# Decay sums of the state-space heads: six matmuls per head, or one table broadcast by DMA

## The chip, the cores and the metric

The kernel runs on one core of a Trainium2 chip, as one program launched once. The metric is the device time of that core in microseconds (us). The engines are TensorE (PE; PEld is its weight load), VectorE (DVE), ScalarE (ACT), GpSimd (POOL) and SyncE (SP), which issues every DMA here.

## The reference, cut to what matters

One layer over 256 prompt tokens and 64 sample tokens, D_MODEL 4096. After an input projection there are 16 attention-like heads ("stick-breaking") and 32 state-space heads of width 64; then an output projection, a gate projection and norms. What the change touches is the decay inside the state-space heads:

```python
dt = softplus(dt_raw + dt_bias)
a = -exp(a_log)
acum = cumsum(dt * a, axis=tokens)          # per head
diff = acum[l] - acum[s]
decay = exp(where(s <= l, diff, -inf))
wts = (C B^T)[l, s] * decay[l, s] * dt[s]
y[l] = sum_s wts[l, s] * x[s]               # + decayed initial state + d_skip * x
```

The reference does this in chunks of 64 with a state between them; the kernel takes all 256 prompt tokens at once, and the 64 sample tokens with the state that is handed in. A prompt and a sample of a head together make a [128 x 512] tile of decays: rows are source tokens s, columns are (s 0-127, l 0-255) | (s 128-255, l 128-255) | (sample s, sample l) | (64 sample l for the initial state).

## The kernel before, in words

**Projections.** All large matrices are taken in column blocks of 256. `project` goes through eight groups of 512 rows; for each, `weights` (L152 to L160) loads a 512 KB tile `raw` by SP, ACT rounds it to `whi` (L158), DVE makes the rest `wlo` (L159), and PE does three float32r matmuls per 128x128 weight tile (L163, L164, L165: `whi*xhi`, `whi*xlo`, `wlo*xhi`), 24 matmuls for each group of rows and block. There are 4 buffers for `raw` and 3 each for `whi` and `wlo`.

**Work behind the projections.** Everything else is written as generators that are put on a list by `start`. After each group of rows, `project` calls `tick`, which takes each generator to its next `yield`. So the small matmuls of the heads stand on PE in blocks between two groups of 24 large matmuls. The engines' programs are put in order ahead of time by the framework's scheduler, and each engine runs its own in order.

**The order of the program.** First three blocks of q, k and v together while x is loaded and transposed (`load_h`; x tiles come from `big()`); then the gate of head pair 0, during which `steps` runs; then four times `ssd_pair`: B and C (two groups of 256 columns), then per group x and z. Head pairs 1 to 7 of the attention follow, then the output projection and the gate.

**State-space heads.** `steps` (L469) makes dt of every token and head, `dta` = dt * a as [128 tokens x 3 windows x 32 heads], its two parts `dtah` and `dtal` in float32r, the decays to the end `dend` and the whole windows' decay `bd`. `ssd_heads` (L614) is started once for each of 16 units of two heads. Its stages: transpose x (`natural`, L557) and scale it to `xdt` and `xde`; per head six DVE multiplications (L636) of the mask `le` by a column of `dtah` or `dtal`, into `gh` and `gl`; the state's matmuls (L640 to L642, once per unit); per head six float32r matmuls (L651 to L656) that sum `gh` and `gl` over tokens with the triangular `gt_r` and the all-ones `ones_r` into a PSUM tile `df`; exp on ACT (L658); times `cb` = masked B^T C on DVE (L659). A tick later y: for each of the unit's two heads four float32 matmuls (L665 to L668) of 64 output rows; head 0 writes PSUM partitions 0 to 63, head 1 partitions 64 to 127. Each float32 matmul stands in the trace as two, called passes here.

`big()` gives [128 x 512] tiles from a ring of 7, used by `load_h`, `steps`, the attention heads and the state-space heads; `small()` gives narrower ones from a ring of 13 with the tag `w`.

Of the kernel before, what the change touches and what calls it, by code (L numbers as in the profile page):

```python
# [30 lines left out]
# Token windows of 128 columns: prompt 0-127, prompt 128-255, and one whose last 64 are the sample.  # L31
WIN = ((0, 128), (128, 256), (192, 320))
# In a row with three convolution columns between prompt and sample.
# [8 lines left out]
def hymba_step(  # L42
# [17 lines left out]
    # what lives in one half of the kernel: the mixers, or the projections behind them  # L60
# [9 lines left out]
    def big(dtype=F32):  # L70
        return pool["wk"].tile([P, 512], dtype, tag="b", name="b", bufs=7)
# [31 lines left out]
    # keeps row > column  # L103
# [5 lines left out]
    # two identities of 32 on top of each other  # L109
# [3 lines left out]
    # Upper bound of the attention scores: huge where a key may be seen, hugely negative elsewhere.  # L113
    # Columns: keys 0-127 x prompt | cache x sample | keys 128-255 x prompt 128-255 | sample keys x sample
    cap = const1.tile([P, 512], F32, name="cap")
    G.memset(cap, -MASKED)
    for c0, n, base in ((0, 128, 0), (320, 128, 0), (448, 64, 64)):
        # keeps column + base - row > 0
        G.affine_select(out=cap[:, c0:c0 + n], in_=cap[:, c0:c0 + n], compare_op=ALU.is_gt,
                        fill=MASKED, base=base, pattern=[[1, n]], channel_multiplier=-1)  # L120
    G.memset(cap[0:64, 448:512], MASKED)
    # 1 where row <= column, by blocks: (0,0) | (0,1) all | (1,1) | sample
# [29 lines left out]
    def weights(src, kg, c0, nk=KG):  # L152
        """nk row tiles of NCOL columns, split exactly into two parts of 12 bits."""
        raw = wp.tile([P, nk, NCOL], F32, tag="raw", name="raw", bufs=4)
        SY.dma_start(raw, src[kg * nk * P:(kg + 1) * nk * P, c0:c0 + NCOL].rearrange("(k p) c -> p k c", p=P))
        hi = wp.tile([P, nk, NCOL], F32R, tag="whi", name="whi")
        lo = wp.tile([P, nk, NCOL], F32R, tag="wlo", name="wlo")
        S.copy(hi, raw)  # L158
        V.tensor_sub(lo, raw, hi.bitcast(F32))  # L159
        return hi, lo  # L160
# [6 lines left out]
    # Work behind a projection, as generators that pause between their stages; projections take  # L167
    # them one step further with each group of rows, so that the tensor engine finds their operands ready.
# [19 lines left out]
    def project(specs, acts, nk=KG, order=range(NG), ticks=True):  # L188
        """Products of column blocks (matrix, first column, PSUM tag), two feature tiles each, with
        all tokens. acts(kg) gives the kg-th group of rows of the activations, in two parts."""  # L190
# [22 lines left out]
    def rsqrt_mean(out, total, n, shape):  # L213
        """out = (total / n + EPS) ** -0.5, with one step of Newton's method."""
# [8 lines left out]
    def factor_of(sqs, n):  # L223
        """The norm's factor of each token, on all partitions, from partial sums of squares."""
# [13 lines left out]
    class Squares:  # L238
        """Sum over `count` feature tiles of squares; the last one stays apart."""
# [3 lines left out]
        def add(self, make):  # L243
            """make(tile, soon) squares the next feature tile."""
# [80 lines left out]
    def gate_in(g):  # L325
        """-g, bounded below as the exponential's argument is above."""
# [4 lines left out]
    def gate_out(es, vals, outs):  # L331
        """out = val / (1 + exp(-g)) for each e of gate_in(g); the quotient by one step of Newton's method."""
# [3 lines left out]
        for e, r in zip(es, rs):  # L336
            # 1 + e, scaled into the logarithm's range
            S.activation(r, e, AF.Ln, scale=2.0 ** -62, bias=tiny)  # L338
# [16 lines left out]
    def put_u(i, ap_mul):  # L355
        """Unit i (16 of each mixer) of the mixed output before its norm."""
# [10 lines left out]
    def to_rows(t, h, dst_p, dst_s, n):  # L367
        """A head's keys or values, back in rows of tokens."""
# [50 lines left out]
    def stick(h, i, q, k, vn, ck, cv, gss):  # L419
# [15 lines left out]
        # softplus(z), and log sigmoid(z) over z  # L435
# [27 lines left out]
    dtah = const1.tile([P, 3, SSDH], F32R, name="dtah")  # L463
    dtal = const1.tile([P, 3, SSDH], F32R, name="dtal")
# [4 lines left out]
    def steps():  # L469
        """dt of each token and head (tokens on partitions), dt * a, and decays."""  # L470
# [8 lines left out]
        # columns of the weights: their first parts, their second parts, nothing  # L479
# [24 lines left out]
        # softplus(r) = max(r, 0) + log1p(e), e = exp(-|r|); log1p(e) = 2 atanh(e / (2 + e))  # L504
# [18 lines left out]
        S.copy(dtah, dta)  # L523
        V.tensor_sub(dtal, dta, dtah.bitcast(F32))
        yield 3
# [12 lines left out]
    def conv(acc, ct, out):  # L538
        """Causal convolution and SiLU of a channel tile; out has 323 columns, the sample's at XS."""
# [74 lines left out]
    def ssd_heads(u, i, xt, made, ys):  # L614
        """Heads 2u and 2u+1: their outputs (transposed) and final states."""
# [14 lines left out]
        wts = []  # L630
        for half in range(2):
            h = 2 * u + half
            gh, gl = big(F32R), big(F32R)
            for out, part in ((gh, dtah), (gl, dtal)):
                for c0, c1, w in ((0, 256, 0), (256, 384, 1), (384, 448, 2)):
                    V.tensor_scalar_mul(out[:, c0:c1], le[:, c0:c1], part[:, w, h:h + 1].bitcast(F32))  # L636
            yield 1
            if half == 0:
                st = aux()
                PE.matmul(st[:, 0:P], xde[:, 0, :], bn[:, 0, :], start=True, stop=False)  # L640
                PE.matmul(st[:, 0:P], xde[:, 1, :], bn[:, 1, :], start=False, stop=True)
                PE.matmul(st[:, P:2 * P], xde[:, 2, :], bn[:, 2, :], start=True, stop=True)  # L642
                so = small((P, 2, P))
                S.copy(so[:, 0, :], st[:, 0:P])
                V.scalar_tensor_tensor(out=so[:, 1, :], in0=h0, scalar=bd[:, u:u + 1], in1=st[:, P:2 * P],
                                       op0=ALU.mult, op1=ALU.add)
                for k, dst in enumerate((ssd_prompt, ssd_sample)):
                    SY.dma_start(dst[0, 0].rearrange("(u a) p n -> (a p) u n", a=2)[:, u, :], so[:, k, :])
            df = aux()
            # sums of dt * a over s < r <= l; the last 64 columns over all r <= l of the sample  # L650
            PE.matmul(df[:, 0:448], gt_r, gh[:, 0:448], start=True, stop=False)  # L651
            PE.matmul(df[:, 0:448], gt_r, gl[:, 0:448], start=False, stop=False)
            PE.matmul(df[:, 128:256], ones_r, gh[:, 256:384], start=False, stop=False)
            PE.matmul(df[:, 128:256], ones_r, gl[:, 256:384], start=False, stop=True)
            PE.matmul(df[:, 448:512], ones_r, gh[:, 384:448], start=True, stop=False)
            PE.matmul(df[:, 448:512], ones_r, gl[:, 384:448], start=False, stop=True)  # L656
            wt = big()
            S.activation(wt, df, AF.Exp)  # L658
            V.tensor_mul(wt, wt, cb)  # L659
            wts.append(wt)  # L660
        yield 1
        y = aux()
        for half, wt in enumerate(wts):
            ph = slice(half * 64, half * 64 + 64)
            PE.matmul(y[ph, 0:256], xdt[:, 0, ph], wt[:, 0:256], start=True, stop=False)  # L665
            PE.matmul(y[ph, 128:256], xdt[:, 1, ph], wt[:, 256:384], start=False, stop=True)  # L666
            PE.matmul(y[ph, 256:320], xdt[:, 2, ph], wt[:, 384:448], start=True, stop=False)
            PE.matmul(y[ph, 256:320], h0t[:, ph], wt[:, 448:512], start=False, stop=True)  # L668
# [158 lines left out]
    def put_pair(fp, gates, es):  # L827
        """Gated embedding of two feature tiles, with the norm's weight."""
# [9 lines left out]
    def to_token_rows(fp, t):  # L838
        """Of each four feature tiles: 512 columns of each half of the prompt's rows, and the sample's rows
        with the first two tiles, then with the last two."""  # L840
# [9 lines left out]
        if half:  # L850
            pt = aux()
            for i in range(2):
                # a transpose writes from the first row on: the last two's, then the first two's over their head
# [8 lines left out]
    # units: a group's rows of half of the prompt, or two groups' rows of the sample  # L862
# [27 lines left out]
    def some_residuals(count):  # L890
        """The first units' residuals, into SBUF ahead of time."""
# [91 lines left out]
```

## Time and profile before

| | before |
|---|---|
| time, median of 3 runs | 2769.45 us (2768.79 to 2770.16) |
| the profiled execution's span | 2768.3 us |
| PE busy | 2741.7 us, 99% |
| DVE busy | 1450.8 us, 52% |
| ACT busy | 1110.9 us, 40% |
| POOL busy | 241.5 us, 9% |
| DMA | 414 MB, 150 GB/s, q1 at 50.2% of 16 engines |

For the profiled execution the page gives the span alone, from the first instruction to the last; the median of the timed runs is 1.15 us longer. A busy engine is one with at least one instruction in it. PE's matmuls overlap, so its time is read from one start to the next, not from the duration of one.

### The profile page before, as it was taken

To read this page: it belongs to the slowest core of one execution; us is meant where nothing else is said; L and a number is where in the kernel's file an instruction comes from. 1 tells how busy PE (TensorE), PEld (TensorE's weight loads), DVE (VectorE), ACT (ScalarE), POOL (GpSimd) and SP (SyncE) were. 2 spreads that over 40 slices of the span, in tenths; PEclk is the share of its full clock that TensorE was granted. 3 is DMA by queue.
4 is the path that set the end of the run, shared out by engine and by line. 5 is a ranking of instruction groups with operands and counts; after the bars stand their busy time and mean duration, and the time that the engine had idled before them with its cause. 6 is when DMAs were issued, how large, how long until landed. Compare 5 with 4: busy or idle time off the path is not lost.

```text
span 2768.3 us, 45230 instructions
## 1 busy us (share of the span) xinstructions
PE 2741.7 (99%) x18710; PEld 2713.2 (98%) x18710; DVE 1450.8 (52%) x2155; ACT 1110.9 (40%) x1551; POOL 241.5 (9%) x327
## 2 busy tenths in 40 slices
PE   9999999999999999999999999999999999999998
PEld 8999999999999999999999999999999989999997
DVE  4566666666666534435354453653333386454453
ACT  5443334433344333424333343543333354444441
POOL 0000010010000000000000000000101032121110
PEclk9999999999999999999999999999999999999997
DMA  7645454454454554555555455555444464444442
GB/s 236 194 120 145 132 149 138 127 164 127 143 148 134 149 153 143 151 149 146 152 143 157 140 150 161 168 162 159 148 150 152 137 191 147 150 144 151 149 142 84
DMA packets 419183, 414.13 MB, mean 150 GB/s; under 512 B 21792, under 2 KB 410784, under 8 KB 418976
## 3 DMA queue, kind: packets, MB, share of 16 engines
q1 hardware_dynamic: 418976, 411.24, 50.2%
q8 instruction: 146, 2.39, 0.3%
q14 instruction: 61, 0.50, 0.0%
HBM read 390.64 MB, written 20.55 MB: 149 GB/s over the span
## 4 chain that ended last, share of the span: by engine, by line
PE 96%; issue 1%; POOL 1%; DMA 1%; DVE 0%; ACT 0%; SPq 0%; DVEq 0%; POOLq 0%; ACTq 0%
PE acc L163 30%; PE acc L165 29%; PE acc L164 29%; POOL ug L817 1%; PE px L876 1%; DMA raw<-in_w_in_dram 1%; PE aux L665 1%; PE aux L372 0%; PE aux L492 0%; PE aux L557 0%; PE aux L847 0%; PE aux L453 0%; PE aux L666 0%; PE aux L426 0%; PE aux L651 0%
## 5 line engine op out<-in xcount | busy, mean ns | idle before, releaser
L163 PE MATMUL acc<-ahi,whi 128*128 128x320 f32 x5632 | 1757.6, 312 | 0.0
L165 PE MATMUL acc<-ahi,wlo 128*128 128x320 f32 x5632 | 1741.6, 309 | 3.6 <-DVE wlo L159 3.6
L164 PE MATMUL acc<-alo,whi 128*128 128x320 f32 x5632 | 1742.2, 309 | 1.3 <-DVE alo L819 1.2
L159 DVE TENSOR_TENSOR wlo<-raw,whi 128x1024 fp32r<-128x1024 f32 (+1 forms) x720 | 888.9, 1236 | 1119.6 <-ACT whi L158 1109.6
L158 ACT CAST whi<-raw 128x1024 fp32r<-128x1024 f32 (+1 forms) x720 | 747.1, 1038 | 1369.3 <-PE acc L164 1328.0
L165 PEld LDWEIGHTS acc<-ahi,wlo 128*128 128x128 f32 x5632 | 1058.5, 188 | 5.4 <-DVE wlo L159 5.4
L164 PEld LDWEIGHTS acc<-alo,whi 128*128 128x128 f32 x5632 | 1059.7, 188 | 2.5 <-DVE alo L819 2.3
L163 PEld LDWEIGHTS acc<-ahi,whi 128*128 128x128 f32 x5632 | 1059.3, 188 | 2.5
L252 POOL TENSOR_TENSOR stat<-stat,w 128x320 f32<-128x320 f32 x88 | 117.5, 1335 | 596.8 <-ACT w L779 404.6
L236 POOL TENSOR_TENSOR w<-ug 128x320 f32<-128x320 f32 x26 | 31.1, 1197 | 947.2 <-DVE ug L457 687.5
L335 ACT ACTIVATE w<-w 128x320 f32<-128x320 f32 (+1 forms) x96 | 45.1, 470 | 101.6 <-DVE w L328 101.5
L342 DVE SCALAR_TENSOR_TENSOR w<-w 128x320 f32<-128x320 f32 (+1 forms) x96 | 51.3, 541 | 16.3 <-ACT w L340 16.3
L236 POOL TENSOR_TENSOR w<-w 128x320 f32<-128x320 f32 x29 | 31.1, 1071 | 296.4 <-DVE w L346 296.4
L550 DVE SCALAR_TENSOR_TENSOR w<-w,vec 128x323 f32<-128x323 f32 x96 | 53.1, 553 | 2.1
L338 ACT ACTIVATE w<-w,tiny 128x320 f32<-128x320 f32 (+1 forms) x96 | 52.3, 560 | 2.9
L340 ACT ACTIVATE w<-w,shift 128x320 f32<-128x320 f32 (+1 forms) x96 | 52.2, 559 | 1.4
L344 DVE SCALAR_TENSOR_TENSOR w<-w 128x320 f32<-128x320 f32 (+1 forms) x96 | 49.6, 529 | 1.2
L545 POOL COPY ctail<-w 128x3 f32<-128x3 f32 x32 | 6.1, 190 | 328.3 <-DVE w L543 328.3
L328 DVE TENSOR_SCALAR w<-acc 128x320 f32<-128x320 f32 x32 | 15.6, 488 | 24.8 <-PE acc L165 24.7
L817 POOL TENSOR_TENSOR ug<-ug,two 128x320 f32<-128x320 f32 x16 | 23.7, 1486 | 43.2 <-DVE ug L816 43.2
L818 ACT CAST ahi<-ug 128x320 fp32r<-128x320 f32 x32 | 14.4, 461 | 25.8 <-POOL ug L817 22.4
L636 DVE TENSOR_SCALAR b<-le,dtah 128x256 fp32r<-128x256 f32 (+2 forms) x96 | 24.7, 292 | 0.0
(270 smaller groups left out, 1476.7 us busy)
## 6 DMA issues: line engine op xcount, KB each, us to landing
raw<-in_w_in_dram SPq DMA_DIRECT2D x448, 512.0 KB, 3.7
raw<-in_w_out_dram SPq DMA_DIRECT2D x128, 512.0 KB, 3.6
raw<-in_w_ple_gate_dram SPq DMA_DIRECT2D x128, 512.0 KB, 3.6
xt_dram<-ug SPq DMA_DIRECT2D x8, 640.0 KB, 6.2
two<-xt_dram SPq DMA_DIRECT2D x16, 320.0 KB, 3.3
b<-in_x_prompt_dram SPq DMA_DIRECT2D x16, 256.0 KB, 4.7
out_dram<-nat SPq DMA_DIRECT2D x32, 128.0 KB, 1.8
raw<-in_w_ple_proj_dram SPq DMA_DIRECT2D x16, 256.0 KB, 2.7
```

Source lines behind the costliest of these rows:

```text
L158: S.copy(hi, raw)
L159: V.tensor_sub(lo, raw, hi.bitcast(F32))
L163: PE.matmul(out, whi, xhi, start=start, stop=False)
L164: PE.matmul(out, whi, xlo, start=False, stop=False)
L165: PE.matmul(out, wlo, xhi, start=False, stop=stop)
L236: G.tensor_mul(sq, t, t)
L252: G.tensor_add(self.sum, self.sum, sq)
L338: S.activation(r, e, AF.Ln, scale=2.0 ** -62, bias=tiny)
L340: S.activation(r, r, AF.Exp, scale=-1.0, bias=shift)
L342: V.scalar_tensor_tensor(out=e, in0=e, scalar=1.0, in1=r, op0=ALU.add, op1=ALU.mult)
L550: V.scalar_tensor_tensor(out=c, in0=ext[:, j:j + XE], scalar=vec3[:, j * 32 + ct:j * 32 + ct + 1], in1=c, op0=ALU.mult, op1=ALU.add)
L817: (G if j % 2 else V).tensor_add(m, m, xt[:, j % 2, :])
```

## The change

Three things are changed in the state-space heads, and one buffer count.

1. `steps` sums `dta` over tokens once for all 32 heads (three float32 matmuls with a triangular matrix `tri`, in which sums start anew every 32 tokens), writes the [32 x 512] table to DRAM (`sums_dram`), and makes a table `off` of [128 x 32 heads x 16] offsets by twenty more small float32 matmuls, in four stages with a `yield` ahead of each.
2. `ssd_heads` no longer makes `gh` and `gl` and no longer runs the six matmuls per head. A DMA on SP broadcasts a head's row of 512 sums to all 128 partitions of a tile `t`; DVE subtracts `off` (one value per 32 columns) and takes the minimum with 0; then exp in place, times `cb` in place.
3. The y matmuls of the two heads alternate, piece by piece, where before all four of head 0 stood ahead of those of head 1.
4. `big()` has 6 buffers, was 7. The comments are dropped.

```diff
     def big(dtype=F32):
-        return pool["wk"].tile([P, 512], dtype, tag="b", name="b", bufs=7)
+        return pool["wk"].tile([P, 512], dtype, tag="b", name="b", bufs=6)
...
-    dtah = const1.tile([P, 3, SSDH], F32R, name="dtah")
-    dtal = const1.tile([P, 3, SSDH], F32R, name="dtal")
+    off = const1.tile([P, SSDH, 16], F32, name="off")
+    sums_dram = dram.tile([SSDH, 512], F32, name="sums_dram")
...
-        S.copy(dtah, dta)
-        V.tensor_sub(dtal, dta, dtah.bitcast(F32))
-        yield 3
+        tri = small((P, P))
+        V.tensor_copy(tri, le[:, 0:P])
+        for c in range(1, 4):
+            G.memset(tri[0:32 * c, 32 * c:32 * c + 32], 0.0)
+        yield 1
+        pt = aux()
+        PE.matmul(pt[0:32, 0:128], dta[:, 0, :], tri, start=True, stop=True)
+        PE.matmul(pt[0:32, 128:256], dta[:, 1, :], tri, start=True, stop=True)
+        PE.matmul(pt[0:32, 256:320], dta[:, 2, :], tri[:, 64:128], start=True, stop=True)
+        sums = big()
...
+        SY.dma_start(sums_dram, sums[0:32, :])
+        pt = aux()
+        acc = pt.rearrange("p (k h) -> p k h", k=16)
+        after = small((P, P))
+        V.tensor_scalar_mul(after, gt, -1.0)
+        for c in range(4):
+            mat = small((P, P))
+            V.tensor_copy(mat, le[:, 0:P])
+            if c:
+                V.tensor_copy(mat[0:32 * c, :], after[0:32 * c, :])
+            early = small((P, P))
+            G.memset(early, 0.0)
+            if c:
+                G.memset(early[0:32 * c, :], -1.0)
+            yield 1
+            PE.matmul(acc[:, c, :], mat, dta[:, 0, :], start=True, stop=True)
+            PE.matmul(acc[:, 8 + c, :], mat, dta[:, 1, :], start=True, stop=True)
+            if c >= 2:
+                PE.matmul(acc[:, 10 + c, :], mat, dta[:, 2, :], start=True, stop=True)
+                PE.matmul(acc[:, 12 + c, :], early, dta[:, 2, :], start=True, stop=True)
+            PE.matmul(acc[:, 4 + c, :], after, dta[:, 0, :], start=True, stop=False)
+            PE.matmul(acc[:, 4 + c, :], early, dta[:, 1, :], start=False, stop=True)
+        V.tensor_copy(off, acc.rearrange("p k h -> p h k"))
...
+        sums = []
         for half in range(2):
-            gh, gl = big(F32R), big(F32R)
-            for out, part in ((gh, dtah), (gl, dtal)):
-                for c0, c1, w in ((0, 256, 0), (256, 384, 1), (384, 448, 2)):
-                    V.tensor_scalar_mul(out[:, c0:c1], le[:, c0:c1], part[:, w, h:h + 1].bitcast(F32))
...
-            PE.matmul(df[:, 0:448], gt_r, gh[:, 0:448], start=True, stop=False)
-            PE.matmul(df[:, 0:448], gt_r, gl[:, 0:448], start=False, stop=False)
-            PE.matmul(df[:, 128:256], ones_r, gh[:, 256:384], start=False, stop=False)
-            PE.matmul(df[:, 128:256], ones_r, gl[:, 256:384], start=False, stop=True)
-            PE.matmul(df[:, 448:512], ones_r, gh[:, 384:448], start=True, stop=False)
-            PE.matmul(df[:, 448:512], ones_r, gl[:, 384:448], start=False, stop=True)
-            wt = big()
-            S.activation(wt, df, AF.Exp)
-            V.tensor_mul(wt, wt, cb)
+            t = big()
+            SY.dma_start(t, sums_dram[2 * u + half:2 * u + half + 1, :].broadcast_to([P, 512]))
+            sums.append(t)
+        yield 1
...
+        for half, t in enumerate(sums):
+            t16 = t.rearrange("p (k c) -> p k c", k=16)
+            V.tensor_sub(t16, t16, off[:, 2 * u + half, :].unsqueeze(2).broadcast_to([P, 16, 32]))
+            V.tensor_scalar_min(t, t, 0.0)
+            S.activation(t, t, AF.Exp)
+            V.tensor_mul(t, t, cb)
         yield 1
         y = aux()
-        for half, wt in enumerate(wts):
-            ph = slice(half * 64, half * 64 + 64)
-            PE.matmul(y[ph, 0:256], xdt[:, 0, ph], wt[:, 0:256], start=True, stop=False)
...
+        for a, b, c, w, first_, last_ in pieces:
+            for half, wt in enumerate(sums):
+                ph = slice(half * 64, half * 64 + 64)
+                PE.matmul(y[ph, a:b], h0t[:, ph] if w == 3 else xdt[:, w, ph], wt[:, c:c + b - a],
+                          start=first_, stop=last_)
```

On PE, around one unit of two heads, before: y of the unit that ends (b_2867 and b_2915 are its two heads' weights, aux_2968 is y), the state's matmuls of the next unit, and the sums of that unit's first head. The large matmuls ahead and behind are left out.

```order
L665 MATMUL aux_2968<-b_2867,nat_2805 64x256
L666 MATMUL aux_2968<-b_2867,nat_2805 64x128
L667 MATMUL aux_2968<-b_2867,nat_2805 64x64
L668 MATMUL aux_2968<-b_2867,w_2486 64x64
L665 MATMUL aux_2968<-b_2915,nat_2805 64x256
...
L640 MATMUL aux_2980<-nat_2447,nat_2923 128x128
...
L651 MATMUL aux_2989<-b_2930,gt_r_102 128x448
...
L656 MATMUL aux_2989<-b_2931,ones_r_89 128x64
```

On PE of the changed kernel, the state's matmuls of a unit and, 24 large matmuls later, its y (b_2871 and b_2873 are the two heads' weights).

```order
L676 MATMUL aux_2905<-nat_2505,nat_2864 128x128
L677 MATMUL aux_2905<-nat_2505,nat_2864 128x128
L678 MATMUL aux_2905<-nat_2505,nat_2864 128x128
...
L700 MATMUL aux_2952<-b_2871,nat_2863 64x256
L700 MATMUL aux_2952<-b_2873,nat_2863 64x256
L700 MATMUL aux_2952<-b_2871,nat_2863 64x128
L700 MATMUL aux_2952<-b_2873,nat_2863 64x128
L700 MATMUL aux_2952<-b_2871,nat_2863 64x64
L700 MATMUL aux_2952<-b_2873,nat_2863 64x64
```

The rows L651 to L656 have no counterpart, and the rows of y alternate between the two heads. L640 to L642, now L676 to L678, stand in a block of their own.

On DVE, in `steps` of the changed kernel, the chain that makes `dta` (L515 and L516 are one step of a polynomial, L522 writes `dta`; the seven steps before and behind are left out). The copies L529, L545, L549 and L551 make `tri`, `after` and the matrices `mat`.

```order
L529 COPY w<-le 128x128
L515 TENSOR_TENSOR w<-w 128x96
L545 TENSOR_SCALAR w<-gt 128x128
...
L549 COPY w<-le 128x128
L516 TENSOR_SCALAR w<-w 128x96
L551 COPY w<-w 32x128
...
L522 SCALAR_TENSOR_TENSOR dta<-dt,w 128x32 x3
L539 COPY b<-aux 32x192
L540 COPY b<-aux 32x64
L159 TENSOR_TENSOR wlo<-raw,whi 128x1024 x2
```

Nine such copies now stand between the first row of the chain and `dta`, none before. On PE the first matmul that reads `dta` stands at the same place as before: 72 large matmuls behind L500 (now L501).

On SP, in the first projection, a piece of the difference: `b` are the x tiles, `dsk` is the d_skip vector spread over partitions (64 rows of 16 single values, twice), `raw` the weights.

```order
-L400 DMA keep<-in_cache_v_dram 128x128
-L478 DMA dsk<-in_d_skip_dram 64x16x1
-L155 DMA raw<-in_w_in_dram 128x4x256
-L293 DMA xt_dram<-ug 128x1280
...
-L478 DMA dsk<-in_d_skip_dram 64x16x1
-L155 DMA raw<-in_w_in_dram 128x4x256 x2
...
+L400 DMA keep<-in_cache_v_dram 128x128
+L479 DMA dsk<-in_d_skip_dram 64x16x1 x2
+L155 DMA raw<-in_w_in_dram 128x4x256
+L293 DMA xt_dram<-ug 128x1280
```

With one x tile less to load early, the second `dsk` moves up to stand right behind the first; before, two x tiles' worth of loads and two `raw` stood between them.

## Rows read from the trace of the kernel before

**Rows 1.** Page: the span, and each engine's busy time, share and instructions.

```profile
span 2768.3 us, 45230 instructions
PE 2741.7 (99%) x18710; PEld 2713.2 (98%) x18710; DVE 1450.8 (52%) x2155; ACT 1110.9 (40%) x1551; POOL 241.5 (9%) x327
```

**Rows 2.** Windows: the state-space stage (PE, PEld, DVE, ACT, POOL; clock, DMA).

```profile
186.00:934.00 748.00, 748.00 (x5201) 738.12 (x5199) 496.12 (x976) 295.49 (x397) 63.92 (x161) 1.00 0.49 140
```

**Rows 3.** Timeline of PE, two heads' sums (start, duration, engine, line, operation).

```profile
267.90 0.45 PE L651 MATMUL aux<-b,gt_r 128*128 128x448 f32 x1
...
268.75 0.39 PE L163 MATMUL acc<-ahi,whi 128*128 128x320 f32 x1
...
272.35 0.37 PE L651 MATMUL aux<-b,gt_r 128*128 128x448 f32 x1
...
273.12 0.55 PE L557 MATMUL aux<-ident,keep 128*128 128x128 f32 x3
```

**Rows 4.** Timeline of PE, y of one unit (x2: both passes in one row).

```profile
277.12 0.65 PE L665 MATMUL aux<-b,nat 128*64 128x256 f32 x2
...
277.82 0.22 PE L667 MATMUL aux<-b,nat 128*64 128x64 f32 x1
277.82 0.43 PE L665 MATMUL aux<-b,nat 128*64 128x256 f32 x1
...
277.93 0.28 PE L668 MATMUL aux<-b,w 128*64 128x64 f32 x2
...
278.64 0.28 PE L668 MATMUL aux<-b,w 128*64 128x64 f32 x2
278.85 0.49 PE L640 MATMUL aux<-nat 128*128 128x128 f32 x2
```

**Rows 5.** Timeline of DVE and PE at the end of `steps` (brackets: idle before, releaser).

```profile
176.15 1.23 DVE L159 TENSOR_TENSOR wlo<-raw,whi 128x1024 fp32r<-128x1024 f32 x1 [0.44 <-ACT whi L158]
...
181.73 0.39 DVE L521 SCALAR_TENSOR_TENSOR dta<-dt,w 128x32 f32<-128x32 f32 x3
...
182.06 0.38 PE L528 MATMUL aux<-dta,gt 128*128 128x32 f32 x2
...
182.84 0.30 PE L535 MATMUL aux<-dta,ones 128*64 128x16 f32 x4
183.07 0.41 PE L163 MATMUL acc<-ahi,whi 128*128 128x320 f32 x1
```

**Rows 6.** Groups by line and shape, DVE (busy us, mean ns of one, idle before).

```profile
L659 DVE TENSOR_TENSOR b<-b 128x512 f32<-128x512 f32 x32 | 22.0, 687 | 2.1 <-ACT b L658 2.1
...
L636 DVE TENSOR_SCALAR b<-le,dtah 128x256 fp32r<-128x256 f32 x32 | 11.1, 347 | 0.0
...
L108 DVE CAST gt_r<-gt 128x128 fp32r<-128x128 f32 x1 | 0.2, 221 | 0.0
```

**Rows 7.** DMA issues (count, KB each, median us to landing).

```profile
b<-in_x_prompt_dram SPq DMA_DIRECT2D x16, 256.0 KB, 4.7
...
w<-in_dt_bias_dram SPq DMA_DIRECT2D x1, 16.0 KB, 3.6
```

**Rows 8.** Waits of SP's queue (total us, times, longest).

```profile
SPq L155 <- DVE wlo L159: 1687.7, 548, 9.6
```

**Rows 9.** Timeline of SP in the first projection.

```profile
55.71 0.66 SPq L478 DMA_DIRECT2D dsk<-in_d_skip_dram  x1
...
59.12 5.57 SPq L275 DMA_DIRECT2D b<-in_x_prompt_dram  x1
...
68.47 0.63 SPq L478 DMA_DIRECT2D dsk<-in_d_skip_dram  x1
69.19 9.73 SPq L155 DMA_DIRECT2D raw<-in_w_in_dram  x2
```

**Rows 10.** Waits of PE (total us, times, longest).

```profile
PE aux L283 <- ACT ug L287: 2.0, 1, 2.0
```

**Rows 11.** Windows: the stretch behind that wait, columns as in rows 2.

```profile
86.20:89.60 3.40, 3.40 (x15) 3.40 (x14) 2.15 (x5) 2.76 (x9) 0.32 (x1) 0.50 1.09 339
```

More of the change, by code (lines that the diff above doesn't have):

```diff
@@ L522, in steps @@
                                    op0=ALU.mult, op1=ALU.mult)
-        S.copy(dtah, dta)
-        V.tensor_sub(dtal, dta, dtah.bitcast(F32))
-        yield 3
+        tri = small((P, P))
[8 more added lines that the diff above has]
+        sums = big()
+        S.copy(sums[0:32, 0:256], pt[0:32, 0:256])
+        V.tensor_copy(sums[0:32, 256:448], pt[0:32, 128:320])
+        V.tensor_copy(sums[0:32, 448:512], pt[0:32, 256:320])
+        SY.dma_start(sums_dram, sums[0:32, :])
[21 more added lines that the diff above has]
+        V.tensor_copy(off, acc.rearrange("p k h -> p h k"))
         pt = aux()
@@ L629, in ssd_heads @@
             V.tensor_mul(split(xde), split(xdt), wide(dend))
-        wts = []
+        sums = []
         for half in range(2):
-            h = 2 * u + half
-            gh, gl = big(F32R), big(F32R)
-            for out, part in ((gh, dtah), (gl, dtal)):
-                for c0, c1, w in ((0, 256, 0), (256, 384, 1), (384, 448, 2)):
-                    V.tensor_scalar_mul(out[:, c0:c1], le[:, c0:c1], part[:, w, h:h + 1].bitcast(F32))
[L637 to L649, printed above, removed]
-            PE.matmul(df[:, 0:448], gt_r, gh[:, 0:448], start=True, stop=False)
-            PE.matmul(df[:, 0:448], gt_r, gl[:, 0:448], start=False, stop=False)
-            PE.matmul(df[:, 128:256], ones_r, gh[:, 256:384], start=False, stop=False)
-            PE.matmul(df[:, 128:256], ones_r, gl[:, 256:384], start=False, stop=True)
-            PE.matmul(df[:, 448:512], ones_r, gh[:, 384:448], start=True, stop=False)
-            PE.matmul(df[:, 448:512], ones_r, gl[:, 384:448], start=False, stop=True)
-            wt = big()
-            S.activation(wt, df, AF.Exp)
-            V.tensor_mul(wt, wt, cb)
-            wts.append(wt)
@@ new lines, in ssd_heads @@
+            t = big()
+            SY.dma_start(t, sums_dram[2 * u + half:2 * u + half + 1, :].broadcast_to([P, 512]))
+            sums.append(t)
+        yield 1
+        st = aux()
+        PE.matmul(st[:, 0:P], xde[:, 0, :], bn[:, 0, :], start=True, stop=False)
+        PE.matmul(st[:, 0:P], xde[:, 1, :], bn[:, 1, :], start=False, stop=True)
+        PE.matmul(st[:, P:2 * P], xde[:, 2, :], bn[:, 2, :], start=True, stop=True)
+        so = small((P, 2, P))
+        S.copy(so[:, 0, :], st[:, 0:P])
@@ new lines, in ssd_heads @@
+        V.scalar_tensor_tensor(out=so[:, 1, :], in0=h0, scalar=bd[:, u:u + 1], in1=st[:, P:2 * P],
+                               op0=ALU.mult, op1=ALU.add)
+        for k, dst in enumerate((ssd_prompt, ssd_sample)):
+            SY.dma_start(dst[0, 0].rearrange("(u a) p n -> (a p) u n", a=2)[:, u, :], so[:, k, :])
+        for half, t in enumerate(sums):
[4 more added lines that the diff above has]
+            V.tensor_mul(t, t, cb)
@@ L661, in ssd_heads @@
         yield 1
         y = aux()
-        for half, wt in enumerate(wts):
-            ph = slice(half * 64, half * 64 + 64)
-            PE.matmul(y[ph, 0:256], xdt[:, 0, ph], wt[:, 0:256], start=True, stop=False)
-            PE.matmul(y[ph, 128:256], xdt[:, 1, ph], wt[:, 256:384], start=False, stop=True)
-            PE.matmul(y[ph, 256:320], xdt[:, 2, ph], wt[:, 384:448], start=True, stop=False)
-            PE.matmul(y[ph, 256:320], h0t[:, ph], wt[:, 448:512], start=False, stop=True)
+        pieces = ((0, 256, 0, 0, True, False), (128, 256, 256, 1, False, True),
+                  (256, 320, 384, 2, True, False), (256, 320, 448, 3, False, True))
```

## The prediction

> **What bounds the kernel now.** I began with the page's busy times: PE is busy for 2741.7 of 2768.3 us [rows 1], DVE for half, ACT for two fifths. A share over the whole span is an average over stages, so I then took the windows of the stage that the change edits, from 186 to 934 us: PE is busy there for 748.00 of 748.00 us at a granted clock of 1.00, that is 2.4 GHz, DVE for 496, ACT for 295, and the DMA engines for 0.49 [rows 2]. PE waits for nothing there. So each microsecond of PE work that goes leaves the time whole, as long as nothing new makes PE wait, and work on the other engines counts only where it delivers late. The reader should take PE's times from one start to the next, as its durations overlap.
>
> **The six matmuls of a head.** In the timeline of PE, a head's first sum starts at 267.90 and the next large matmul at 268.75: 0.85 us. The other head's starts at 272.35 and the next transposes at 273.12: 0.77 [rows 3]. The mean is 0.81, and 32 heads give -26.0 us.
>
> **The y matmuls in turn.** Before, y runs from 277.12 to the next unit's state matmuls at 278.85, 1.73 us [rows 4]. Head 0's last matmul, at 277.93, is two passes that start 0.06 apart (277.87 to 277.93 is one such step), so a head alone takes from 277.12 to about 278.05, 0.93 us. The two together take less than twice that, because at the boundary head 1's first pass starts at 277.82, in the same instant as head 0's L667 and ahead of two later passes of head 0 (277.87 and 277.93). The heads use different halves of the array's columns, and the row shows both at work. If the new order lets them run side by side all along, a unit's y takes about 0.93 + 0.09 for the gap to the next block, and saves 0.70; the other bound is that no more overlaps than now, 0. If passes overlap but none starts ahead of one that stands before it, I lay them out by width: both passes of one piece at head 0, with head 1 one pass behind. At every step to a narrower piece head 0 waits for the start of head 1's wider second pass, and the unit takes 1280 column steps where a head alone has 1024, so 0.93 x 1.25 = 1.16 and a saving of 0.47. I take 0.55 of a microsecond, nearer to that than to the full 0.70, since an overtaking is seen only over a few short passes: 16 units give -8.8 us, with 0 and -11.2 as bounds.
>
> The Trainium skill bears on this ("TensorE: Matmul & The Clock Gate", Part 3: Packing small matmuls — row/col tiling, "The mechanism"): tiles in different column groups overlap, but matmuls start and end strictly in program order. The overlap agrees with this trace; the order doesn't, since 277.82 is ahead of 277.87. By the rule the term would be 16 x 0.47 = 7.5 us, by the row up to 11.2.
>
> **The new matmuls of `steps`.** There are 23 small float32 matmuls, which is 46 passes. The nearest rows are those of `steps` itself: five matmuls of the same 128 rows and of 16 to 64 columns are 10 passes between 182.06 and 183.07, 0.10 us each [rows 5]. So 46 cost 4.6, and a little for the three wide ones of 64 to 128 columns: +5.0 us, between 4 and 6. They sit between large matmuls and nothing hides them.
>
> **`dta` comes later.** Before, `dta` is written from 181.73 and PE's L528 starts at 182.06 with no wait and no slack [rows 5]. After, nine DVE copies stand inside the chain that ends with `dta`, while PE meets its first reader behind the same 72 large matmuls. The nearest row is a 128x128 cast of 221 ns [rows 6]: nine are 2.0 us. DVE had 0.44 us of idle time in this stretch (ahead of L159 at 176.15) [rows 5], which leaves about +1.5 us of waiting on PE. The bounds are 0, if the copies fit in the latencies between dependent steps, and 3.7, if a half-clock stretch follows like the one in the next part.
>
> **The first projection.** The `dsk` loads (64 rows of 16 single values on all partitions) block SP's queue: the x tile's issue behind the first, at 59.12, takes 5.57 us, and two `raw` behind the second, at 69.19, take 9.73 [rows 9]. Later, PE waits 2.0 us for `ug` (L283 on L287) [rows 10], which I followed back to a late `raw`; behind it a stretch of 3.4 us ran at a granted clock of 0.50, 1.2 GHz [rows 11], which lost half of that, 1.7. So this place costs 3.7 us before. With one buffer less the second `dsk` stands right behind the first, and the `raw` behind both meets the two blocks in a row, while later there is none. I estimate a wait of 3.5 and the same 1.7 behind it: 5.2 in place of 3.7, +1.5 us. The bounds are -3.7, if the four `raw` buffers hide the lump, and +8, if the second block (9.73, less the 1.7 that stands in both) comes fully on top.
>
> **What I cost at nothing.** DVE, per head: six multiplications, twice 347, 280 and 248 ns, and one of 687 go [rows 6], 2.4 us; a subtraction, a minimum and a multiplication of 128x512 come, at most 3 x 0.69 = 2.1. ACT keeps one exp per head. Their cover is PE's 24 large matmuls of about 3.5 us for each `tick`, and DVE's idle third of the stage. Without it a unit's y would come about 1 us late. The broadcasts: 32 of 256 KB. The nearest rows are the x tiles of the same size, 4.7 us to landing, and the spread of `dt_bias`, 3.6 us [rows 7]; they are long rows, as here, not single values as `dsk`. At 0.49 of the DMA time there is room. Each broadcast has a wait on SP for its tile, and `raw` loads queue behind it; but SP waits 1687.7 us in all for L159 to release `raw`, up to 9.6 at once [rows 8], so `raw` runs that far ahead and a few microseconds on SP don't reach PE. By the order, the first unit's broadcasts are issued about six groups ahead of their use; a later one waits for the y that frees its tile, which comes at about the place where they are due.
>
> **The sum.** -26.0 - 8.8 + 5.0 + 1.5 + 1.5 = -26.8, so a span of 2741.5 us against 2768.3. The median of the runs shown is 1.15 above that span, so the time would be about 2743 us. By its own bounds this case reaches from 2736 to 2748.
>
> **The rivals.** (a) *The halves don't overlap more than now.* For: the overtaking seen is of short passes only; against: they did overlap. +8.8, so 2751.5. (b) *The two `dsk` together stall PE harder*, +8 in place of +1.5: 2749. For: 5.57 and 9.73 us of blocked queue; against: four `raw` buffers. (c) *The new chain is late.* Broadcast, subtraction, minimum, exp and product follow one another, where before the sums came from PE; if y waits 1 us in each of 16 units, 2759. For: tiles of the ring of six come free only when y has read them; against: DVE's idle third. (d) *Slower: the broadcasts clog SP's queue as `dsk` does.* If each unit's pair costs PE what the second `dsk` did, 3.7 us, that is 59 us: 2802. It decides from 26.8 / 16 = 1.7 us per unit. For: both spread a row over all partitions; against: [rows 7], where long rows land in 3.6 to 4.7 us. (e) *No change.* A stream of weights that bound the stage would swallow the gain; PE's 748.00 of 748.00 speaks against it: 2769.
>
> **How the numbers follow.** About 0.2%, 5.5 us, can be told from no change here. The chances are: the forecast 0.56, (a) 0.12, (b) 0.12, (c) 0.09, (d) 0.05, (e) 0.03, and 0.03 for something better than its range. The range from 2734 to 2756 holds the forecast, (a) and (b), and leaves out (c), (d), (e): 0.83. Faster are all but (d) and (e), 0.92; the same 0.03; slower 0.05.
>
> **What would show it.** In the stage from the end of `steps` to the last y, PE idle at zero, and the rows of L651 to L656 gone. At y, L700 starting in pairs, and about 1.2 us (1.02 to 1.26) from its first start to the next block; 1.7 is (a), and pairs in which a narrow pass of head 0 never starts ahead of a wide one of head 1 are the strict order. In `steps`, 46 passes more, some 5 us, and a wait of PE at the first reader of `dta`, on DVE. Between 60 and 90 us a wait that leads back to `raw`, and its length. SP's waits at `raw` still on L159, and the broadcasts' landing near 5 us; if they take 10 or more and SP waits elsewhere, (d). PE waits at L700 on DVE are (c). I'd be wrong above all if a wait appears in the stage at every unit, since each tenth of a microsecond there counts 16 times, or if the scheduler's order lets a broadcast wait on SP for a tile longer than `raw` is ahead.

## The result and the profile after

The changed kernel takes 2740.88 us (median of 4 runs, 2739.43 to 2743.11) against 2769.8 for the kernel before on the same chip: a ratio of 0.9894, with a 95% interval from 0.988 to 0.9908. The profiled execution's span is 2741.3 us; 2741.5 was forecast. That the spans fit so closely is partly luck: the gains came out 3.9 us larger than forecast and the losses 2.0, and shifts that no term covers took most of the rest. The profiled execution was also the slowest of the four runs. By the medians the kernel gained 28.9 us where 26.8 were forecast, and the time, about 2743 us by the forecast, was 2 us lower.

The page of the changed kernel first: span, and each engine's busy time, share and instructions.

```profile
span 2741.3 us, 44859 instructions
PE 2700.0 (98%) x18564; PEld 2672.8 (97%) x18564; DVE 1439.8 (53%) x2038; ACT 1109.6 (40%) x1551; POOL 242.4 (9%) x337
```

PE's busy time fell by 41.7 us against [rows 1] and the span by 27.0, so PE has more idle time than before, 14.7 us. It isn't in the state-space stage. The windows of the same stretch as in [rows 2] (PE, PEld, DVE, ACT, POOL; clock, DMA share, GB/s):

```profile
186.00:934.00 748.00, 747.96 (x5281) 740.11 (x5280) 503.35 (x875) 306.08 (x414) 64.96 (x165) 1.00 0.56 159
```

PE idles for 0.04 us in all, and the DMA share went from 0.49 to 0.56 with the broadcasts. The waits of PE over the whole span (total us, times, longest) say where a part of the 14.7 us is:

```profile
PE aux L283 <- DMA b<-in_x_prompt_dram: 5.7, 2, 3.1
PE acc L165 <- DVE wlo L159: 4.2, 4, 2.0
PE aux L142 <- POOL le L124: 2.6, 1, 2.6
PE aux L283 <- DVE ug L289: 1.6, 1, 1.6
```

L283 transposes the x tiles of the first projection. Neither L700 (y) nor the first reader of `dta` is in that answer. Most of the idle time lies at the end of the program, behind the last large matmul, where the windows show this, first of the kernel before and then of the changed one:

```profile
2722.00:2768.00 46.00, 33.42 (x195) 32.36 (x193) 19.35 (x35) 6.02 (x14) 0.87 (x1) 0.60 0.33 115
2695.00:2741.00 46.00, 22.33 (x196) 21.76 (x194) 18.73 (x35) 6.17 (x14) 0.87 (x1) 0.76 0.33 115
```

In the kernel before, PE is busy for 33.42 of them at a mean granted clock of 0.60, in the changed kernel for 22.33 at 0.76. The same matmuls ran there at the lower clock for longer, and their later end cost nothing: PE's last matmul ends 13 us ahead of the end of the span before and 24 us ahead after, with the outputs' transfers behind it. From the start of the last large matmul to the end of the span it is 46.3 us before and 46.1 after. So 11 of the 41.7 us of busy time are no gain.

Both traces hold the same 17088 large matmuls of lines L163 to L165. Setting the start of each against the start of the same one of before gives the account by stage (us from the span's start):

| large matmul, counted from 0 | before | after | difference so far |
|---|---|---|---|
| 24 | 18.4 | 19.2 | +0.8 |
| 408, first projection past `load_h` | 90.3 | 95.8 | +5.5 |
| 860, ahead of the sums in `steps` | 177.9 | 183.4 | +5.5 |
| 960, behind `steps` | 193.7 | 204.5 | +10.8 |
| 5400, behind the last y | 930.3 | 902.4 | -27.9 |
| 17087, the last | 2722.0 | 2695.2 | -26.8 |

So the stages gave +4.7 and +5.3 and then -38.7. The 0.8 at the top lies in the first loads. Over the runs below this place varies from -0.4 to +1.3, with seven buffers as well as with six, so it is no sign of the change. The 1.0 us lost again behind the stage comes in two steps, of 0.3 at 1766 us and of 0.7 at 2275 us of the kernel before, the second at L165.

The timeline of PE at one unit's y, which answers to [rows 4] (x12: passes in one row):

```profile
282.14 0.31 PE L165 MATMUL acc<-ahi,wlo 128*128 128x320 f32 x1
282.38 0.99 PE L700 MATMUL aux<-b,nat 128*64 128x256 f32 x12
283.20 0.29 PE L700 MATMUL aux<-b,w 128*64 128x64 f32 x4
283.41 0.33 PE L596 MATMUL aux<-ident,keep 128*128 128x128 f32 x1
```

From 282.38 to 283.41 is 1.03 us, where before it was 1.73. That is a head alone and the gap: the halves run side by side all along. In the single records of this block, the two heads' first passes start 7 ns apart, then their second passes 0.27 later and again 7 ns apart, and so to the end.

### The profile page after: what moved, and what is told of

The parts are those of the page before. It is cut to its first block, busy times and chain, and to the rows that moved or that the text cites. A ratio compares the mean times of both kernels' runs of the same rounds, so it can differ in the third digit from the quotient of the medians.

```text
span 2741.3 us, 44859 instructions
## 1 busy us (share of the span) xinstructions
PE 2700.0 (98%) x18564; PEld 2672.8 (97%) x18564; DVE 1439.8 (53%) x2038; ACT 1109.6 (40%) x1551; POOL 242.4 (9%) x337
## 2 busy tenths in 40 slices
DMA packets 423837, 422.57 MB, mean 154 GB/s; under 512 B 22320, under 2 KB 411312, under 8 KB 423632
## 4 chain that ended last, share of the span: by engine, by line
PE 95%; issue 2%; POOL 1%; DMA 1%; DVE 0%; ACT 0%; SPq 0%; DVEq 0%; POOLq 0%; ACTq 0%
PE acc L163 30%; PE acc L165 30%; PE acc L164 30%; POOL ug L850 1%; PE aux L700 1%; PE px L909 0%; PE aux L372 0%; PE aux L493 0%; DMA raw<-in_w_in_dram 0%; PE aux L596 0%; PE aux L880 0%; PE aux L453 0%; PE aux L285 0%; PE aux L283 0%; PE aux L426 0%
## 5 line engine op out<-in xcount | busy, mean ns | idle before, releaser
L163 PE MATMUL acc<-ahi,whi 128*128 128x320 f32 x5632 | 1757.7, 312 | 0.0
L165 PE MATMUL acc<-ahi,wlo 128*128 128x320 f32 x5632 | 1741.9, 310 | 4.2 <-DVE wlo L159 4.2
L159 DVE TENSOR_TENSOR wlo<-raw,whi 128x1024 fp32r<-128x1024 f32 (+1 forms) x720 | 888.2, 1235 | 1088.9 <-ACT whi L158 1081.9
L165 PEld LDWEIGHTS acc<-ahi,wlo 128*128 128x128 f32 x5632 | 1058.8, 188 | 6.0 <-DVE wlo L159 6.0
L163 PEld LDWEIGHTS acc<-ahi,whi 128*128 128x128 f32 x5632 | 1059.6, 188 | 2.7
L690 ACT ACTIVATE b<-b 128x512 f32<-128x512 f32 x32 | 19.6, 625 | 16.6 <-DVE b L689 16.6
```

Source lines behind the costliest of these rows:

```text
L163: PE.matmul(out, whi, xhi, start=start, stop=False)
L165: PE.matmul(out, wlo, xhi, start=False, stop=stop)
```

## The experiments

Times are medians, ratios go against the kernel before on the same chip.

**The y matmuls in turn, alone.** In the kernel before, with nothing else changed:

```diff
-        for half, wt in enumerate(wts):
-            ph = slice(half * 64, half * 64 + 64)
-            PE.matmul(y[ph, 0:256], xdt[:, 0, ph], wt[:, 0:256], start=True, stop=False)
...
+        for a, b, c, w, first_, last_ in pieces:
+            for half, wt in enumerate(wts):
+                ph = slice(half * 64, half * 64 + 64)
...
```

> The kernel before, with the y matmuls of the two heads in turn and nothing else. My theory: the halves run fully side by side, a unit's y with its gap falls from 1.73 to 1.03 us, 16 units give -11.2 us, so about 2758.5 against 2769.7. Rival, strict program order of starts: 16 x 0.47 = 7.5, about 2762. Rival, the gain in the stage comes from elsewhere (the state's matmuls moving to their own block): 2769.7, no change.

Measured: 2759.65 us against 2771.15, ratio 0.9958 [0.9945, 0.997]; 11.5 us less. Between the two traces the large matmuls gain 0.70 us at each of the 16 units and nothing else in the stage. The timeline of PE at a unit's y:

```profile
278.17 0.99 PE L668 MATMUL aux<-b,nat 128*64 128x256 f32 x12
278.99 0.29 PE L668 MATMUL aux<-b,w 128*64 128x64 f32 x4
279.20 0.49 PE L640 MATMUL aux<-nat 128*128 128x128 f32 x2
```

From y to the state's matmuls it is again 1.03 us. The order alone gives the whole 11.2; moving the state's matmuls to their own block, which this kernel doesn't do, isn't needed for it.

**The old order of y in the changed kernel.**

```diff
-        for a, b, c, w, first_, last_ in pieces:
-            for half, wt in enumerate(sums):
+        for half, wt in enumerate(sums):
+            for a, b, c, w, first_, last_ in pieces:
```

> The changed kernel with y's four matmuls of head 0 ahead of those of head 1 again. My theory: +11.2 us, about 2752, of 2740.9. Rival, strict order: +7.5, about 2748. Rival, the order of y does nothing here: 2740.9.

Measured: 2752.94 us, ratio 0.9936 [0.9923, 0.9948], where the changed kernel had 0.9894. That is 12 us more, 0.70 at each of 16 units by the trace. So this part of the change adds up with the others, and strict order, which would give 7.5, is out by both runs.

**How far a pass overtakes.** Two more orders of y in the changed kernel: two pieces of a head at a time, and three and then one.

```diff
-            for half, wt in enumerate(sums):
+        for k, half, wt in ((k, half, wt) for k in (0, 2) for half, wt in enumerate(sums)):
+            for a, b, c, w, first_, last_ in pieces[k:k + 2]:
```

> The changed kernel with y's order of two pieces of head 0 (256 and 128 columns), the same two of head 1, then the two narrow ones of head 0 and of head 1. My theory, from the boundary of the kernel before, where a pass of head 1 started ahead of three passes of head 0: a pass overtakes three, so the halves still run side by side all along and the time is 2741. Rival, starts in strict program order: head 1 begins with the last pass of head 0's second piece, a unit takes about 1.7 us, 2752.

> The changed kernel with y's order of three pieces of head 0, three of head 1, then the last of each. If a pass overtakes three and no more, head 1 begins with head 0's second piece, about 0.48 us late, and a unit takes about 1.5 us in place of 1.03: 2748. If it overtakes any number: 2741. In strict order: 2752.

Measured: two pieces at a time 2742.11 us, ratio 0.9898 [0.9884, 0.9911], the same as in turn within the spread; three 2749.87 us, ratio 0.9925 [0.9911, 0.9939], and by the large matmuls 0.48 us more at each of the 16 units than in turn. The timeline of PE with two pieces at a time, and then with three:

```profile
280.83 1.04 PE L700 MATMUL aux<-b,nat 128*64 128x256 f32 x12
281.65 0.34 PE L700 MATMUL aux<-b,w 128*64 128x64 f32 x4
281.92 0.55 PE L596 MATMUL aux<-ident,keep 128*128 128x128 f32 x3
```

```profile
282.81 1.24 PE L700 MATMUL aux<-b,nat 128*64 128x256 f32 x9
283.78 0.27 PE L700 MATMUL aux<-b,w 128*64 128x64 f32 x1
283.89 0.27 PE L700 MATMUL aux<-b,nat 128*64 128x128 f32 x1
...
284.32 0.55 PE L596 MATMUL aux<-ident,keep 128*128 128x128 f32 x3
```

With three pieces the unit takes 1.51 us, as worked out. In its single records head 1's first pass starts 0.49 us behind head 0's, together with the first pass of head 0's second piece; three passes of head 0 that stand ahead of it start later, at 0.59, 0.70 and 0.76. Head 0's last piece, at 283.78, likewise starts ahead of three passes of head 1, at 283.89, 284.00 and 284.05. With two pieces only three passes stand between, and a unit takes 1.09 us by its timeline, 0.06 more than in turn. All this is as if a pass of the idle half could start ahead of three waiting ones and not of a fourth; what in the engine sets the three, these runs don't tell.

**The six matmuls, alone.** The kernel before without L651 to L656, so that the sums are left out of the weights and exp reads `gh` and `gl` in their place:

```diff
-            PE.matmul(df[:, 0:448], gt_r, gh[:, 0:448], start=True, stop=False)
...
-            PE.matmul(df[:, 448:512], ones_r, gl[:, 384:448], start=False, stop=True)
-            S.activation(wt, df, AF.Exp)
+            S.activation(wt[:, 0:448], gh[:, 0:448].bitcast(F32), AF.Exp)
+            S.activation(wt[:, 448:512], gl[:, 0:64].bitcast(F32), AF.Exp)
```

> The kernel before without the six matmuls per head; exp reads gh and gl in their place, so that the weights are not the reference's, and everything else, the multiplications on DVE too, stays. My theory: each head's block costs PE 0.86 us with its edges, 32 heads give -27.4 us, about 2742.5. Rival, my forecast's price of 0.81: 2744. Rival, the removal alone does nothing because the DVE work behind it is the bound of the stage: 2770.

Measured: 2742.63 us against 2770.48, ratio 0.9901 [0.9887, 0.9914]; 27.8 us less. By the large matmuls it is 27.1 in the stage, between 0.82 and 0.86 at each of the 32 blocks. Its windows of the stage:

```profile
186.00:934.00 748.00, 748.00 (x5190) 738.75 (x5189) 509.06 (x994) 308.16 (x442) 66.16 (x162) 1.00 0.51 146
```

All the DVE multiplications are still made, and PE never waits. So this gain is PE's alone; it doesn't need the other work that DVE does in the changed kernel.

**The buffer count, alone.** The kernel before with six big buffers:

```diff
-        return pool["wk"].tile([P, 512], dtype, tag="b", name="b", bufs=7)
+        return pool["wk"].tile([P, 512], dtype, tag="b", name="b", bufs=6)
```

> The kernel before with six buffers for the big tiles in place of seven, and nothing else; by the order its two loads of the d_skip vector then stand one behind the other, as in the changed kernel. My theory: the whole loss of 5.6 us up to 107 us comes from that, so about 2775 (2774 to 2776). Rival: the loss belongs to other parts of the change, and this is 2769.7. A second rival: the sums' tiles gh and gl, which the old kernel takes from the same ring, run short as well and PE waits in the state-space stage: above 2778.

Measured: 2774.79 us against 2771.15, ratio 1.0014 [1.0005, 1.0023]. It is slower by 3.6 us at the median, where 5.6 was expected; in the traces its large matmuls lose 4.4 between the 24th and the 408th, where the changed kernel loses 4.7. The expectation had counted the changed kernel's shift at the top with it. The timeline of SP in this kernel, in the first projection:

```profile
56.03 1.38 SPq L478 DMA_DIRECT2D dsk<-in_d_skip_dram  x2
58.58 4.32 SPq L155 DMA_DIRECT2D raw<-in_w_in_dram  x1
63.03 7.39 SPq L293 DMA_DIRECT2D xt_dram<-ug  x1
70.54 6.51 SPq L275 DMA_DIRECT2D b<-in_x_prompt_dram  x2
```

And the same place of the changed kernel:

```profile
55.54 1.38 SPq L479 DMA_DIRECT2D dsk<-in_d_skip_dram  x2
58.09 6.50 SPq L155 DMA_DIRECT2D raw<-in_w_in_dram  x1
64.73 3.50 SPq L293 DMA_DIRECT2D xt_dram<-ug  x1
68.34 7.95 SPq L275 DMA_DIRECT2D b<-in_x_prompt_dram  x2
```

The two `dsk` stand together in both, and the next four issues take until about 77. The windows of the changed kernel show what passes meanwhile, and what PE pays:

```profile
58.00:76.00 18.00, 18.00 (x118) 16.82 (x118) 9.08 (x15) 11.03 (x25) 0.00 (x0) 1.00 0.09 17
82.00:84.00 2.00, 0.00 (x0) 0.00 (x0) 0.81 (x1) 1.04 (x1) 0.00 (x0) 1.00 1.02 303
84.00:94.00 10.00, 7.93 (x25) 5.51 (x26) 5.17 (x9) 6.13 (x13) 0.63 (x2) 0.51 1.03 353
60.00:100.00 40.00, 35.67 (x210) 32.03 (x209) 15.33 (x21) 18.65 (x38) 0.63 (x2) 0.87 0.54 177
```

For 18 us the DMA engines moved 17 GB/s. After that PE idled from 82 to 84, and the ten microseconds behind ran at a granted clock of 0.51, the lower of its two levels (1.2 GHz), with two microseconds more of idling inside them.

**`dsk` as rows.** The same vector, loaded at the same place of the queue in rows of 32 consecutive values, in the changed kernel and in the one before:

```diff
+    drow = const1.tile([P, SSDH], F32, name="drow")
...
-        dpair = d_skip[0].rearrange("(u h) -> h u", h=2)
+        SY.dma_start(drow, d_skip[0:1, :].broadcast_to([P, SSDH]))
         for half in range(2):
-            SY.dma_start(dsk[half * 64:(half + 1) * 64, :], dpair[half:half + 1, :].broadcast_to([64, 16]))
+            V.tensor_copy(dsk[half * 64:(half + 1) * 64, :],
+                          drow.rearrange("p (u h) -> p h u", h=2)[half * 64:(half + 1) * 64, half, :])
```

> The changed kernel with the d_skip vector loaded once as 128 rows of 32 consecutive values in place of twice 64 rows of 16 single ones, at the same place of the queue; two small DVE copies pick the values out. My theory, that the 2048 packets of 4 bytes block the queue: no wait and no half clock between 60 and 100 us, which takes back the 4.7 us that the change lost there and the 3.7 that the kernel before lost, so -8.4 us, about 2732.5. Rival, the ring of six itself makes the x tiles late: the same wait stays, 2740.9, or a part of it, 2738.

> The kernel before with the d_skip vector loaded as 128 rows of 32 consecutive values, as in the changed kernel's variant. My theory: the wait of 2.0 us at L283 and the half clock behind it go, -3.7 us, about 2766.5 against 2770.3. Rival: that wait had another cause, 2770.

Measured: in the changed kernel 2732.67 us, ratio 0.9861 [0.9848, 0.9875], 8.2 us less than the changed kernel and 8.3 by the large matmuls between the 24th and the 408th; in the kernel before 2766.41 against 2771.03, ratio 0.9985 [0.9976, 0.9994], with 3.7 less between the same two large matmuls. The changed kernel with rows, the timeline of SP and the windows:

```profile
54.99 0.43 SPq L478 DMA_DIRECT2D drow<-in_d_skip_dram  x1
57.54 0.38 SPq L155 DMA_DIRECT2D raw<-in_w_in_dram  x1
58.91 0.33 SPq L293 DMA_DIRECT2D xt_dram<-ug  x1
```

```profile
60.00:100.00 40.00, 40.00 (x263) 37.16 (x261) 20.41 (x29) 24.00 (x50) 0.63 (x2) 1.00 0.70 214
```

The issue behind it takes 0.38 in place of 6.50, PE never idles from 60 to 100 and the clock stays at 1.00. The ring still has six buffers, so it isn't the ring itself that makes the x tiles late, it is what the smaller ring moved together. The Trainium skill ("DMA: Bandwidth & Descriptors", Rules for kernel authors) has the rule for this: a transfer whose last dimension isn't contiguous becomes one descriptor for each element, and should be laid out so that it is. The traces agree: the profile counts 22320 packets under 512 B with the single values and 20384 with the rows, 1936 fewer (2048 values against 128 rows would be 1920), and the 18 us of blocked queue go with them.

**The broadcasts twice.** The changed kernel with each broadcast issued two times:

```diff
             SY.dma_start(t, sums_dram[2 * u + half:2 * u + half + 1, :].broadcast_to([P, 512]))
+            SY.dma_start(t, sums_dram[2 * u + half:2 * u + half + 1, :].broadcast_to([P, 512]))
```

> The changed kernel with each of the 32 broadcasts issued twice into the same tile, the second behind the landing of the first, so that SP is held about 5 us longer for each. My theory: raw is up to 10 us ahead, PE sees little of it: 2741 to 2745. Rival, that the broadcasts hold up the weights already: at 3.7 us for each unit 2741 + 59 = 2800; anything above 2768 would make the change a loss at twice the broadcasts.

Measured: 2741.71 us, ratio 0.9896 [0.9882, 0.9909], no slower than the changed kernel. SP's waits (total us, times, longest), and the DMA issues (count, KB, us to landing):

```profile
SPq L155 <- DVE wlo L159: 1581.6, 540, 9.7
...
SPq L673 <- DMA b<-sums_dram: 43.5, 32, 4.0
```

```profile
b<-sums_dram SPq DMA_DIRECT2D x64, 256.0 KB, 4.3
```

SP now stands for 43.5 us behind the first broadcasts, and takes it out of its waits for L159, which in the changed kernel were these:

```profile
SPq L155 <- DVE wlo L159: 1637.4, 549, 9.6
```

PE sees none of it: it is busy for 747.95 of the stage's 748.00 us.

**A better version.** The changed kernel with `dsk` as rows, and the offsets' matmuls of windows 0 and 1, which share a stationary matrix, made as one:

```diff
-            PE.matmul(acc[:, c, :], mat, dta[:, 0, :], start=True, stop=True)
-            PE.matmul(acc[:, 8 + c, :], mat, dta[:, 1, :], start=True, stop=True)
+            PE.matmul(acc[:, c:c + 9:8, :], mat, dta[:, 0:2, :], start=True, stop=True)
```

> The changed kernel with d_skip loaded as rows, and with the matmuls of the offsets that share one stationary matrix (windows 0 and 1) made as one of 64 columns, so that 8 of the 46 new passes go. My theory: 2732.7 less 8 x 0.11 = 0.9, about 2731.8, which is about the spread of the runs. Rival: a pass of 64 columns costs twice one of 32, and nothing more is gained: 2732.7.

Measured: 2732.15 us, ratio 0.9862 [0.9848, 0.9875]. In the traces the four blocks of `steps` cost PE 0.88 us less together, 0.11 for each of the 8 passes, so a pass of 64 columns costs there what one of 32 does. The medians, 2732.15 and 2732.67, don't tell the two apart. Both beat the changed kernel.

## Why the prediction was right, step by step

| step | forecast | measured | from |
|---|---|---|---|
| six matmuls per head | -26.0 | -27.5 | the stage's -38.7 less the -11.2 of y; alone -27.1 by the large matmuls, -27.8 by the medians |
| y in turn | -8.8 | -11.2 | 0.70 per unit; -11.5 alone |
| new matmuls of `steps` | +5.0 | +5.3 | large matmuls 860 to 960 |
| `dta` later | +1.5 | 0.2 at most, inside the +5.3 | start of L534 |
| first projection | +1.5 | +4.7 | large matmuls 24 to 408 |

**What bounds the kernel** held: each microsecond of PE work that went out of the stage came out of the time, and PE's idle time in it is 0.04 us.

**The six matmuls** were priced from the first sum to the next matmul, 0.85 and 0.77 in [rows 3]. The second price is too low. In the run without them the large matmuls gain 0.85 and 0.82 at these two heads, and 0.85 and 0.86 at the two of the next unit. In the changed kernel what is left for a head is 0.86, which makes 27.5 us for the 32 heads against 27.1 in that run. Where these 0.4 us come from isn't shown.

**y in turn** reached the full bound. The step that was too careful was to read the overtaking at 277.82 in [rows 4] as something of a few short passes; in the orders that ran it is a reach of three passes, wide ones (256 and 128 columns, two pieces at a time) as well as narrow ones, and in turn a pass overtakes one. Rival (a), no more overlap than now, and strict order are both out by the four orders of y that ran.

**The matmuls of `steps`**: 0.11 us a pass where 0.10 was taken. Of the ten passes in [rows 5] the last four, L535, use 64 columns of the array each and start in pairs 7 ns apart, which brought the mean down; the six before them start mostly 0.11 apart, as the new ones do.

**`dta` later** was wrong. The nine copies are there, but they cost the chain 0.04 us each and not 0.22. The timeline of DVE in the kernel before, at the chain's first row, and of DVE and PE in the changed kernel:

```profile
172.81 0.20 DVE L508 TENSOR_SCALAR w<-w 128x96 f32<-128x96 f32 x1
```

```profile
178.27 0.20 DVE L509 TENSOR_SCALAR w<-w 128x96 f32<-128x96 f32 x1
...
181.37 0.21 DVE L516 TENSOR_SCALAR w<-w 128x96 f32<-128x96 f32 x1
181.49 0.21 DVE L551 COPY w<-w 32x128 f32<-32x128 f32 x1
181.63 0.24 DVE L515 TENSOR_TENSOR w<-w 128x96 f32<-128x96 f32 x1
...
187.11 0.38 DVE L522 SCALAR_TENSOR_TENSOR dta<-dt,w 128x32 f32<-128x32 f32 x3
```

```profile
187.08 0.31 PE L163 MATMUL acc<-ahi,whi 128*128 128x320 f32 x1
187.43 0.38 PE L534 MATMUL aux<-w,dta 128*32 128x128 f32 x2
```

From L509 to `dta` it is 8.84 us. In the kernel before the same stretch is no shorter: 8.92 from 172.81 to 181.73 [rows 5]. But those 8.92 hold the 0.44 us in which DVE stood idle ahead of L159 [rows 5], and the changed kernel has no such wait, with two L159 inside the chain as before. Without them it is 8.48, so the copies cost 0.36 us in all, and the wait that is gone covers it. Each step of the chain waits for the one ahead, and 181.37, 181.49, 181.63 shows a copy starting and the next step following 0.26 behind its predecessor, the copy between them. The forecast named copies that fit between dependent steps as its lower bound and took the price of a copy alone on DVE, which is a price for a queue that is full, not for a chain of dependent steps. Its other premise, the same 72 large matmuls ahead of the first reader, doesn't hold either: in the traces L528 starts behind 72 of them, counted from L500, and L534 behind 70, counted from L501. L534 starts 0.35 us behind the large matmul ahead of it, L528 started 0.15 behind its own, so PE may have waited for 0.2 us at most.

**The first projection** is the term that was mis-sized, and rival (b), by its mechanism, is what happened, at +4.7 us where it said +8. The blocked queue was as forecast, but it reached PE in two waits: 2.6 us for an x tile that SP issued late, which the forecast didn't have, and then 1.6 for `ug`, which leads back to `raw`. The price of the clock wasn't: with the wait at 1.7 us of half clock behind it, as in [rows 11], the sum came to 5.2 for this place, while it costs 8.4 (the 3.7 of before and 4.7). The windows show 4.3 us of idling from 60 to 100, where 3.5 was forecast, and a half-clock stretch of some ten microseconds, with further idling inside it, in place of one of 3.4. So about 4.1 us went to the clock. The run with six buffers alone shows the same loss without the rest of the change, and the run with `dsk` as rows takes all of it back.

**What was costed at nothing** held. SP's waits for L159 were the cover of the broadcasts, and a doubled broadcast still fits under them, so rival (d) is far off: the point of 1.7 us per unit isn't reached with twice the transfers. L700 is in no wait of PE, so rival (c) fell too. The broadcasts land in 4.8 us:

```profile
b<-sums_dram SPq DMA_DIRECT2D x32, 256.0 KB, 4.8
```

Against the sum: the gains were larger than forecast by 3.9 us and the losses by 2.0, so the terms as measured give -28.7. The span shows -27.0, with the 0.8 at the top and the 1.0 behind the stage, which the forecast had no term for.

## What to carry to other kernels

Where PE never waits in a stage, the time is the sum of its matmuls, so work that can be computed once and spread by long-row transfers is worth moving, and it is the queue's spare waiting time that has to be shown for it. Independent matmuls that fill different column halves belong next to each other in program order, with at most three passes between, by what ran here. A buffer count changes the order of loads elsewhere: look at what the scheduler moves next to what, and at transfers of single values first, since here 8 KB of them blocked a queue for 18 us.

## What the runs showed of the hardware

- A float32 pass for the idle half of the array starts ahead of up to three passes that stand before it; with five waiting ahead of it, it started 0.49 us late, when three were left.
- Loads of 2048 single values held the DMA queue at 17 GB/s for 18 us; as 128 rows of 32 values, the next issue took 0.38 us.
- Nine copies in a chain of dependent DVE steps cost it 0.36 us together: 8.84 us with them, 8.92 without, of which 0.44 was a wait of another instruction ahead in the queue. The nearest row of one by itself [rows 6] took 0.22.
- The wait for late data costs twice: 4.3 us of idling in the first projection brought about 4.1 us more, with ten microseconds at a granted clock of 0.51 (1.2 GHz).
